# Hybrid encoder trunk: modulation blocks moved from GpSimd to VectorE and TensorE, squares of y kept in pairs, and a mixed block order for the last state-space group

## The chip, the cores and the metric

The kernel runs on one core of a Trainium2 chip. Its time is device time in microseconds (us), the median over runs of the same program. The engines that matter are TensorE (PE, with its weight loads PEld), VectorE (DVE), ScalarE (ACT), GpSimd (POOL), and the queue of SyncE (SP) that issues most transfers. Each engine works through its own instructions in program order, and waits for another engine's results where it needs them.

## The reference, cut to what matters

Two layers over a sequence of 1024 tokens with a width of 1024, in fp32. Layer 0 mixes tokens by dilated window attention with a partial rotary embedding, layer 1 by a bidirectional Mamba-2 state-space mixer of inner width 2048 in eight groups.

```python
cond = silu(c)
for i in range(2):
    mod = cond @ mod_w[i] + mod_b[i]                 # 1024 -> 3072
    shift, scale, gate = split(mod, 3)
    hn = rms_norm(x, norm_w[i]) * (1 + scale) + shift
    if i == 0: y = dilated_attention_mixer(hn, ...)  # (o * silu(z)) @ w_out
    else:      y = bi_ssd_mixer(hn, ...)             # below
    x = x + gate * y
return rms_norm(x, final_norm_w)

# end of bi_ssd_mixer
y = (y_f + y_b + xs * d_skip).reshape(b, s, 2048) * silu(z)
return rms_norm(y, norm_w) @ w_out                   # 2048 -> 1024
```

## The kernel before

Features lie on the 128 partitions and tokens along the free axis, so x is eight tiles (`xt[kt]`) of 128 x 1024. Dense products are made to fp32 accuracy from three matmuls: each operand is split into a high part (a rounded copy, made by ScalarE) and a low part (the difference, made by VectorE), and TensorE sums high x high, high x low, low x high. One such triple (lines 376 to 378 in `mm3`, 1004 to 1006 in `out_items`) covers 128 x 128 weights and 512 tokens. Two triples, for both halves of the tokens, are called a half-step below. The main loop of the kernel is written as lists of such steps, into which the other work is woven.

The start is in `layer0`. The squares of x are made by ScalarE, some are merged by VectorE, and summed over partitions by matmuls with ones, which gives the sum `ss[h]` for each half h of the tokens. From it the inverse root `r[h]` comes as ScalarE's exp(-0.5 ln) and one Newton step on VectorE. The modulation of layer 0 is needed at the same time: shift and scale of feature tile kt are blocks 2kt and 2kt + 1 of 24. A block is a tile of 128 x 1024 (eight 128 x 128 pieces of the modulation weights, `mod_load`). Its product with silu(c), called `cond`, is made before in three stages: all eight pieces are multiplied by their column of `cond` (`mod_acc`; even blocks from 2 on by ScalarE in eight scalings, line 169; blocks 0, 1 and all odd ones by GpSimd in one multiply, line 173), the eight pieces are summed to two (an add of 512 and one of 256 elements, here called a half-sum; on VectorE at line 867 or on GpSimd at line 177), and `mod_fin` sums over the partitions with one-column matmuls (line 197) and forms `modv` and the scale `gs`.

With them `hn_tile` makes the normed tile of a feature tile: x times `gs` times r on VectorE (line 287), the high part with the shift on ScalarE (line 293), the low part on VectorE (line 294). The loop over kt then has eight steps. In each, TensorE makes 18 dense matmuls (three blocks q, k, v of the first head pair, two halves of the tokens, three matmuls each), and the others prepare the tile of the next step, the weights' high and low parts (`w_split`, lines 271 and 272) and modulation blocks of later steps. Loads of modulation blocks stand in the queue of SP two blocks at a time, three pairs ahead of their use.

The tables of the rotary embedding (`rope_tables`) are a long row of small operations of 192 columns. `NT` says how many of them VectorE does at given places of the start. After step 5 of the loop the rest goes to GpSimd.

Layer 1 runs over eight groups. `block_order` sets the order of a group's six projection blocks (x0, x1, B, C and the gates z0, z1); `group_dense` gives a group's projection steps and `ssd_items` those of its scan, a state part (`A1`, `A2`) and then eight chunks (`B0`, `B1`, `M`, `B2`), and `balance` weaves such a list with the projection blocks of the next group, so that each dense half-step stands where the ratio of TensorE's to VectorE's planned time wants it. An item is (length, function, TensorE's us, VectorE's us).

Beside the last group (g = 7) run the first 14 steps of the out-projection (`out1`, `first`) instead of a next group's blocks; such a step has 12 matmuls. Here y is fetched from DRAM tile by tile (`fetch`), and `prep` squares it (ScalarE, or GpSimd for the first three, line 1554), adds the square to a sum on GpSimd (line 1558), and makes the high part (ScalarE, line 1561) and the low part (VectorE, line 1562). The sum of squares over the partitions follows in `sums`. `B2` also ends with gate multiplies on GpSimd (line 1495).

Of the kernel before, what the change touches and what calls it, by code (L numbers as in the profile page):

```python
# [17 lines left out]
P = 128  # L18
# [73 lines left out]
class Trunk:  # L92
# [97 lines left out]
    def mod_fin(self, i, b, *accs):  # L190

        nc = self.nc
        p = self.bank("a2", [P, H2])
        for k, acc in enumerate(accs):
            n = acc.shape[1]
            for c in range(0, n, P):
                nc.tensor.matmul(p[:, k * P:k * P + 1], acc[:, c:c + P], self.ones[:, :1], start=c == 0, stop=c + P == n)
        m = self.modv[i]
        for k in range(len(accs)):
            c = slice(b + k, b + k + 1)  # L200
            nc.vector.tensor_add(m[:, c], p[:, k * P:k * P + 1], self.vec[:, 16 + 24 * i + b + k:17 + 24 * i + b + k])
            if b + k < 16 and (b + k) % 2:
                d = (b + k) // 2
                nc.vector.scalar_tensor_tensor(self.gs[i][:, d:d + 1], m[:, c], 1.0,
                                               self.vec[:, 64 + 8 * i + d:65 + 8 * i + d], op0=OP.add, op1=OP.mult)

# [134 lines left out]
    def block_order(self, g):  # L341

        return (0, 4, 1, 2, 3, 5) if 0 < g < 7 else tuple(range(6))
# [469 lines left out]
    def layer0(self):  # L813
# [33 lines left out]
        self.w_dma(3)  # L847

# [19 lines left out]

        def fin(j):
            self.mod_fin(0, 2 * j, *[mw.pop(2 * j + s)[:, :2 * P] for s in range(2)])  # L870
# [18 lines left out]
        mods(0, nc.gpsimd, 1)  # L889
        mods(1, nc.gpsimd, 1)  # L890
# [24 lines left out]
        fin(0)  # L915
        prep(0)
        self.w_split(1)
        mods(4, nc.scalar)
        mods(5, nc.gpsimd)
        self.finish()  # L920
        self.flush()
        half(2)
        half(4)
        accs = [[self.acc() for _ in range(2)] for _ in range(2)] + [[self.bank("a0", [P, H2], 2) for _ in range(2)]]
        evac = self.evac0 = self.attn_evac(0)
        for kt in range(KT):
            load(kt + 4)
            if 3 < kt + 4 < KT:
                self.w_dma(kt + 4)
            if kt + 3 < KT:  # L930
                mods(2 * kt + 6, nc.scalar)
                mods(2 * kt + 7, nc.gpsimd)
            for m in range(3):
                if m == 0 < kt < KT - 1:
                    fin(kt + 1)
                self.mm3(accs[m], self.whl[kt], slice(m * P, m * P + P), [self.hn[n][kt] for n in range(2)],
                         kt == 0, kt == KT - 1)
                if kt == KT - 1:
# [456 lines left out]
    def ssd_items(self, g):  # L1395
# [119 lines left out]
        if g == 7:  # L1515
            items.append((1500, lambda: None, 0, 0))
# [10 lines left out]
    def out1(self, tail):  # L1527
# [3 lines left out]
        xin, x2, cut, ybuf = {}, {}, {}, {}  # L1531
        ys, st = [{} for _ in range(2)], [{} for _ in range(2)]

        def fetch(r, kt):
            if (r, kt) in cut or (r, kt) in ybuf or kt > 15:
                return
            buf = ybuf[r, kt] = self.big()
            if kt < 14:
                nc.sync.dma_start(buf[:, :H2], self.yd[kt][:, H2 * r:H2 * r + H2])

        def prep(r, kt):
# [67 lines left out]
        def sums(r, a):  # L1609
# [5 lines left out]
            def total():  # L1615
                ys[r]["s"] = self.all_sum(ys[r], 0, H2, self.acc())
# [4 lines left out]
            return [(0.5, out), (1, total), (1, start)]  # L1621

        def first(ps):
            m = tail[0][:]
            for i in range(4):
                m.insert(len(m) - 10 + 2 * i, (1, lambda i=i: prep(0, i)))
            weave(m + [(2600, f) for _, f in ps[0][:14]], tail[1])
            for _, f in ps[1][:2]:
                f()
            for kt in (14, 15):  # L1630
                prep(0, kt)
            for _, f in ps[1][2:4]:
                f()
            self.phase("w3")
# [163 lines left out]
```

## Time and profile before

| | |
|---|---|
| time, median of 3 runs | 1859.21 us (1858.36 to 1860.43) |
| the profiled execution's own time | 1857.47 us |
| its span | 1855.5 us |
| TensorE busy | 1777.3 us (96%) |
| PE weight loads busy | 1453.4 us (78%) |
| VectorE busy | 1420.6 us (77%) |
| ScalarE busy | 956.6 us (52%) |
| GpSimd busy | 328.0 us (18%) |

The busy times are shares of one profiled execution's span. The shares are means over stages of different kinds: a stage in which an engine is nearly always busy can stand beside one in which it waits. So the stages are read one by one, from windows (the busy time of each engine in a stretch) and timelines (an engine's instructions in order; equal ones in a row are joined, and the second number is their time together). Instructions that reach the hardware as several are listed several times: a one-column matmul of the program shows as two. PEclk is the granted clock of TensorE as a share of full speed (2.4 GHz; the lower level is 1.2). "[9.59 <-ACT big L293]" says that the engine was idle for 9.59 us before the instruction, and that the last thing it waited for was ScalarE's write to a tile `big` at line 293.

### The profile page before, as it was taken

To read this page: it belongs to the slowest core of one execution; us is meant where nothing else is said; L and a number is where in the kernel's file an instruction comes from. 1 tells how busy PE (TensorE), PEld (TensorE's weight loads), DVE (VectorE), ACT (ScalarE), POOL (GpSimd) and SP (SyncE) were. 2 spreads that over 40 slices of the span, in tenths; PEclk is the share of its full clock that TensorE was granted. 3 is DMA by queue.
4 is the path that set the end of the run, shared out by engine and by line. 5 is a ranking of instruction groups with operands and counts; after the bars stand their busy time and mean duration, and the time that the engine had idled before them with its cause. 6 is when DMAs were issued, how large, how long until landed. Compare 5 with 4: busy or idle time off the path is not lost.

```text
span 1855.5 us, 28487 instructions
## 1 busy us (share of the span) xinstructions
PE 1777.3 (96%) x10050; PEld 1453.4 (78%) x10050; DVE 1420.6 (77%) x3219; ACT 956.6 (52%) x2095; POOL 328.0 (18%) x493
## 2 busy tenths in 40 slices
PE   5899999999999999999999999999999999798997
PEld 2678788878788888788878788888888878676787
DVE  7966578766755655666687989899898989897975
ACT  5454445544444544544435656565656565565632
POOL 4611112112211221010110101010101010233310
PEclk7899999999999999999999999999999999999998
DMA  6242234322412131173313243433323342344542
GB/s 249 94 122 90 84 103 129 99 84 87 120 47 58 56 80 55 59 229 136 100 41 97 69 118 82 114 89 93 100 83 108 80 111 78 114 133 140 187 160 96
DMA packets 99733, 193.65 MB, mean 104 GB/s; under 512 B 15624, under 2 KB 23048, under 8 KB 99592
## 3 DMA queue, kind: packets, MB, share of 16 engines
q1 hardware_dynamic: 86600, 167.32, 29.7%
q0 software_dynamic: 12288, 23.86, 4.7%
q8 instruction: 79, 1.29, 0.3%
q10 hardware_dynamic: 704, 0.66, 0.1%
q14 instruction: 62, 0.51, 0.1%
HBM read 169.00 MB, written 16.48 MB: 100 GB/s over the span
## 4 chain that ended last, share of the span: by engine, by line
PE 72%; DVE 17%; ACT 4%; issue 3%; DMA 3%; SPq 0%; ACTq 0%; DVEq 0%; POOL 0%
PE acc L376 16%; PE acc L378 15%; PE acc L377 15%; PE a L1487 3%; PE a L1425 2%; DVE wlo L272 2%; PE a L719 2%; PE a L1004 2%; PE a L1005 2%; PE a L1006 2%; DVE big L1336 2%; PE a L704 2%; PE acc L1006 2%; PE acc L1004 2%; PE acc L1005 2%
## 5 line engine op out<-in xcount | busy, mean ns | idle before, releaser
L376 PE MATMUL acc<-big,whi 128*128 128x512 f32 (+1 forms) x1520 | 631.2, 415 | 13.0 <-ACT big L293 12.4
L377 PE MATMUL acc<-big,whi 128*128 128x512 f32 (+1 forms) x1520 | 595.3, 392 | 2.7 <-DVE big L294 2.6
L378 PE MATMUL acc<-big,wlo 128*128 128x512 f32 (+1 forms) x1520 | 595.3, 392 | 0.3 <-DVE wlo L272 0.3
L376 PEld LDWEIGHTS acc<-big,whi 128*128 128x128 f32 x1520 | 288.0, 189 | 78.6 <-issue 15.8
L378 PEld LDWEIGHTS acc<-big,wlo 128*128 128x128 f32 x1520 | 287.5, 189 | 64.3 <-DVE wlo L272 1.2
L377 PEld LDWEIGHTS acc<-big,whi 128*128 128x128 f32 x1520 | 288.7, 190 | 53.0 <-DVE big L294 6.1
L272 DVE TENSOR_TENSOR wlo<-wraw,whi 128x512 fp32r<-128x512 f32 (+1 forms) x297 | 214.1, 726 | 83.1 <-ACT whi L271 80.1
L271 ACT CAST whi<-wraw 128x512 fp32r<-128x512 f32 (+1 forms) x302 | 181.3, 612 | 85.5 <-PE a L1005 27.3
L695 ACT ACTIVATE sm<-sm,nb 128x256 f32<-128x256 f32 (+1 forms) x192 | 89.3, 466 | 194.9 <-DVE nb L693 192.2
L1336 DVE SCALAR_TENSOR_TENSOR big<-acc,cv,big 128x512 f32<-128x512 f32 (+1 forms) x248 | 169.2, 741 | 6.5 <-ACT big L1328 6.5
L1495 POOL TENSOR_TENSOR big<-big,yt 128x128 f32<-128x128 f32 x128 | 65.3, 531 | 586.7 <-DVE yt L1491 586.6
L1457 ACT ACTIVATE E<-E,nacb 128x128 f32<-128x128 f32 x256 | 81.8, 391 | 143.1 <-DVE E L1449 129.4
L706 DVE COPY pt<-a 128x512 f32<-128x512 f32 (+1 forms) x96 | 57.6, 600 | 73.2 <-PE a L704 73.1
L690 DVE CUSTOM_DVE_ANT_0 sm<-a,cst 128x256 f32<-128x256 f32 (+1 forms) x192 | 64.9, 375 | 60.3 <-PE a L685 60.0
L1004 PE MATMUL a<-big,whi 128*128 128x256 f32 (+1 forms) x304 | 99.2, 326 | 0.0
L1006 PE MATMUL a<-big,wlo 128*128 128x256 f32 (+1 forms) x304 | 98.2, 323 | 0.1
L1005 PE MATMUL a<-big,whi 128*128 128x256 f32 (+1 forms) x304 | 97.9, 322 | 0.0
L1005 PE MATMUL acc<-big,whi 128*128 128x512 f32 x224 | 88.9, 397 | 5.9 <-DVE big L1562 3.1
L592 POOL DMA_DIRECT2D rt<-kT x92 | 50.3, 561 | 243.0 <-ACT kT L532 145.8
L1006 PE MATMUL acc<-big,wlo 128*128 128x512 f32 x224 | 89.5, 399 | 3.2 <-DVE wlo L272 2.4
L1004 PE MATMUL acc<-big,whi 128*128 128x512 f32 x224 | 90.5, 404 | 0.0
L1328 ACT ACTIVATE big<-acc,cv 128x512 f32<-128x512 f32 x62 | 44.5, 770 | 86.4 <-PE acc L378 76.0
(254 smaller groups left out, 3181.7 us busy)
## 6 DMA issues: line engine op xcount, KB each, us to landing
wraw<-in_win SPq DMA_DIRECT2D x186, 256.0 KB
acs<-acsd SPq DMA_DIRECT2D x64, 512.0 KB
wraw<-in_wout SPq DMA_DIRECT2D x112, 256.0 KB
big<-in_modw SPq DMA_DIRECT2D x48, 512.0 KB
yd<-big POOLq DMA_DIRECT2D x14, 512.0 KB, 4.4
big<-yd SPq DMA_DIRECT2D x28, 256.0 KB
vT<-mix POOLq DMA_DIRECT2D x20, 256.0 KB, 4.2
big<-in_xT SPq DMA_DIRECT2D x8, 512.0 KB
```

Of the source, the lines that this page charges most:

```text
L271: self.nc.scalar.copy(dst_hi, src)
L272: self.late.append((lambda: self.lo_engine.tensor_sub(dst_lo, src, dst_hi.bitcast(F32)), tile))
L376: mm(o, hi[:, cols], x_[:, t0:t0 + n], start=first, stop=False, **kw)
L377: mm(o, hi[:, cols], x_[:, H2 + t0:H2 + t0 + n], start=False, stop=False, **kw)
L378: mm(o, lo[:, cols], x_[:, t0:t0 + n], start=False, stop=last, **kw)
L695: nc.scalar.activation(sm[:, h, :W], sm[:, h, :W], AF.Exp, bias=nb[:, h:h + 1], scale=0.125, accum_out=stat[:, h, 1, i:i + 1])
L1004: mm(o, hi[:, c], x[:, t:t + n], start=kt == 0 and (n == H2 or m % 2 == 0), stop=False, **kw)
L1005: mm(o, hi[:, c], x[:, H2 + t:H2 + t + n], start=False, stop=False, **kw)
L1006: mm(o, lo[:, c], x[:, t:t + n], start=False, stop=kt == nkt - 1, **kw)
L1336: nc.vector.scalar_tensor_tensor(y[:, lo:hi], a[:, lo + o:hi + o], w[:, cv, k:k + 1], y[:, lo:hi], op0=OP.mult, op1=OP.add)
L1457: nc.scalar.activation(E[:, h], E[:, h], AF.Exp, bias=self.nacb[:, c, 4 * g + h:4 * g + h + 1])
L1495: nc.gpsimd.tensor_mul(z, z, t[:, r])
```

## The change

It has three parts. First, the modulation of layer 0. GpSimd takes no block any more. Block 0 is multiplied and half-summed by VectorE. Blocks 1, 2, 3, 4, 6, 10 and 14 (`pe`) aren't multiplied at all: TensorE multiplies their eight pieces with the eight columns of `cond`, summing over the partitions and the pieces in one go. The other eight (`act`) are scaled by ScalarE and half-summed by VectorE. `mod_fin` gives way to a new `fin`. Two more pairs of blocks are loaded ahead. The order of the start changes too: the first weights' split stands ahead of the norm, and the first half's Newton step and normed tile come before the second half's.

Second, the squares of y for the first half of the tokens. y is fetched in pairs of tiles. ScalarE makes all squares and writes them into pair tiles; GpSimd adds the pair tiles (`add_pair`), three of them inside the list of steps and four behind it; the last sum takes two matmuls. The first four tiles of y are prepared, and the next ones fetched, a few places earlier, and the list is woven by `balance` instead of `weave`. The total is asked for two places later.

Third, the last group's blocks stand in the mixed order of the others, and an empty item of its list gets a planned 2.0 us of VectorE.

```diff
     def block_order(self, g):
 
-        return (0, 4, 1, 2, 3, 5) if 0 < g < 7 else tuple(range(6))
+        return (0, 4, 1, 2, 3, 5) if g else tuple(range(6))
...
+        load(4)
+        load(5)
...
+
         def fin(j):
-            self.mod_fin(0, 2 * j, *[mw.pop(2 * j + s)[:, :2 * P] for s in range(2)])
+
+            p = self.bank("a0", [P, 2, P], 2) if j < 2 else self.bank("a2" if j % 2 else "a3", [P, 2, P])
+            for k in (1, 0):
+                w = mw.pop(2 * j + k)
+                n = KT if 2 * j + k in pe else 2
+                for c in range(n):
+                    x = self.cond[:, c:c + 1] if n == KT else self.ones[:, :1]
+                    nc.tensor.matmul(p[:, k, :1], w[:, c * P:c * P + P], x, start=c == 0, stop=c == n - 1)
+            m = self.modv[0]
+            c = slice(2 * j, 2 * j + 2)
+            nc.vector.tensor_add(m[:, c], p[:, :, 0], self.vec[:, 16 + 2 * j:18 + 2 * j])
+            nc.vector.scalar_tensor_tensor(self.gs[0][:, j:j + 1], m[:, 2 * j + 1:2 * j + 2], 1.0,
+                                           self.vec[:, 64 + j:65 + j], op0=OP.add, op1=OP.mult)
 
         turn(NT[0])
         for kt in range(KT):
...
         for h in range(2):
             merge(6, slice(h * H2, h * H2 + H2))
             total(sq[6], False, True, (h,))
+        mods(0, nc.vector, 1)
+        half(0)
+        self.w_split(0)
+        self.flush()
         r, v = [[self.u(t, [P, H2], F32, n) for _ in range(2)] for t, n in (("pt", 4), ("sm", SM))]
...
-            half(h)
-        self.w_split(0)
-        mods(2, nc.scalar)
-        mods(3, nc.gpsimd)
-        def prep(kt):
+        self.w_split(1)
+
+        def prep(kt, hs=range(2)):
             if kt < KT:
-                for h in range(2):
+                for h in hs:
                     self.hn_tile(0, kt, h * H2, H2, xt[kt][:, h * H2:h * H2 + H2], r[h], self.hn)
 
         for h in range(2):
             nc.vector.scalar_tensor_tensor(u[h], u[h], -0.5, v[h], op0=OP.mult, op1=OP.mult)
             nc.vector.scalar_tensor_tensor(r[h], u[h], 1.5, r[h], op0=OP.add, op1=OP.mult)
-        fin(0)
-        prep(0)
-        self.w_split(1)
-        mods(4, nc.scalar)
-        mods(5, nc.gpsimd)
+            if h == 0:
+                fin(0)
+            prep(0, (h,))
+            self.flush()
...
+        mods(5, nc.scalar)
         self.finish()
         self.flush()
-        half(2)
-        half(4)
+        fin(1)
...
-            load(kt + 4)
+            if kt < 2:
+                load(kt + 6)
...
-                mods(2 * kt + 6, nc.scalar)
-                mods(2 * kt + 7, nc.gpsimd)
...
+            for b in (2 * kt + 4, 2 * kt + 5):
+                if b in act:
+                    half(b)
             prep(kt + 1)
             self.w_split(kt + 2)
+            for b in (2 * kt + 6, 2 * kt + 7):
+                if b in act:
+                    mods(b, nc.scalar)
...
-            items.append((1500, lambda: None, 0, 0))
+            items.append((1500, lambda: None, 0, 2.0))
...
+        def add_pair(k):
+
+            for n in range(2):
+                c = slice(n * H2, n * H2 + H2)
+                nc.gpsimd.tensor_add(pairs[0][:, c], pairs[0][:, c], pairs[k][:, c])
+            pairs[k] = None
...
-            if r == 0 and kt < 3:
-                nc.gpsimd.tensor_mul(sq, y, y)
             else:
-                nc.scalar.activation(sq, y, AF.Square)
-            if kt:
+                sq = buf[:, H2:]
+            nc.scalar.activation(sq, y, AF.Square)
+            if kt and r:
                 nc.gpsimd.tensor_add(ys[r]["sq"][:, :H2], ys[r]["sq"][:, :H2], sq)
...
-            for i in range(4):
-                m.insert(len(m) - 10 + 2 * i, (1, lambda i=i: prep(0, i)))
-            weave(m + [(2600, f) for _, f in ps[0][:14]], tail[1])
+            for at, f, k in ((1, prep, 3), (2, prep, 2), (3, fetch, 4), (4, prep, 1), (6, prep, 0), (8, fetch, 2), (12, fetch, 0)):
+                m.insert(max(len(m) - at, 0), (1, lambda f=f, k=k: f(0, k), 0, 0.7 if f is prep else 0))
+            balance(m + [(2600, f, 2.76, 1.4) for _, f in ps[0][:14]], tail[1])
+            add_pair(4)
+            add_pair(5)
```

How instructions stand on three engines, before and after. VectorE at the start, from the first half-sums to the first normed tile, before (`sm` and `pt` hold the variance and the inverse root, `big_104` and `big_106` are blocks 0 and 1, `kT` is the normed tile):

```order
L867 TENSOR_TENSOR big_104<-big_104 128x512
L867 TENSOR_TENSOR big_104<-big_104 128x256
L900 TENSOR_SCALAR sm_210<-a_14_87 128x512
L867 TENSOR_TENSOR big_106<-big_106 128x512
L867 TENSOR_TENSOR big_106<-big_106 128x256
L913 SCALAR_TENSOR_TENSOR big_211<-big_211,sm_209 128x512
L914 SCALAR_TENSOR_TENSOR pt_207<-big_211,pt_207 128x512
L913 SCALAR_TENSOR_TENSOR big_211<-big_211,sm_210 128x512
L914 SCALAR_TENSOR_TENSOR pt_208<-big_211,pt_208 128x512
L201 TENSOR_TENSOR modv_6_75<-a_50_242,vec_65 128x1 x2
L204 SCALAR_TENSOR_TENSOR gs_8_77<-modv_6_75,vec_65 128x1
L287 SCALAR_TENSOR_TENSOR kT_250<-big_88,gs_8_77,pt_207 128x512
```

And after, the same place:

```order
L173 TENSOR_TENSOR big_104<-big_104,cond_73 128x1024
L852 TENSOR_TENSOR big_104<-big_104 128x512
L852 TENSOR_TENSOR big_104<-big_104 128x256
L255 TENSOR_TENSOR wlo_217<-wraw_108,whi_216 128x384
L903 TENSOR_SCALAR sm_222<-a_13_86 128x512
L903 TENSOR_SCALAR sm_223<-a_14_87 128x512
L914 SCALAR_TENSOR_TENSOR big_224<-big_224,sm_222 128x512
L915 SCALAR_TENSOR_TENSOR pt_220<-big_224,pt_220 128x512
L869 TENSOR_TENSOR modv_6_75<-a_57_240,vec_65 128x2
L870 SCALAR_TENSOR_TENSOR gs_8_77<-modv_6_75,vec_65 128x1
L270 SCALAR_TENSOR_TENSOR kT_253<-big_88,gs_8_77,pt_220 128x512
L255 TENSOR_TENSOR wlo_234<-wraw_114,whi_233 128x384
```

The multiply of block 0 (line 173 in both) is new here, block 1's half-sum is gone, and the first half's Newton step and normed tile stand ahead of the second half's Newton step.

GpSimd at the start, before (`big_104`, `big_106`, `big_112` are blocks 0, 1 and 3):

```order
L173 TENSOR_TENSOR big_104<-big_104,cond_73 128x1024
L173 TENSOR_TENSOR big_106<-big_106,cond_73 128x1024
L173 TENSOR_TENSOR big_112<-big_112,cond_73 128x1024
L177 TENSOR_TENSOR big_112<-big_112 128x512
L177 TENSOR_TENSOR big_112<-big_112 128x256
L173 TENSOR_TENSOR big_118<-big_118,cond_73 128x1024
L177 TENSOR_TENSOR big_118<-big_118 128x512
L177 TENSOR_TENSOR big_118<-big_118 128x256
```

And after, where `vT` and `V` hold the rotary tables:

```order
L464 TENSOR_TENSOR vT_82<-vT_82,vT_83 128x192 x2
L464 TENSOR_TENSOR vT_83<-vT_83 128x192
L471 TENSOR_TENSOR V_84<-V_84,vT_82 128x192 x2
L471 TENSOR_TENSOR V_84<-V_84,vT_83 128x192
L475 TENSOR_SCALAR vT_82<-V_84 128x192
L477 TENSOR_SCALAR vT_83<-vT_82 128x192
L479 TENSOR_SCALAR vT_83<-vT_83 128x192
L481 TENSOR_TENSOR V_84<-vT_82,vT_83 128x192
```

The multiplies are gone, and the rotary tables' second part, which stood behind the last of them, is the first work.

GpSimd in the last group, before, from the first squares (line 1554) and accumulations (line 1558) of y to the first gate multiplies (line 1495):

```order
L1554 TENSOR_TENSOR big_15779<-big_15777 128x512
L1554 TENSOR_TENSOR big_15837<-big_15837 128x512
L1558 TENSOR_TENSOR big_15779<-big_15779,big_15837 128x512
L1554 TENSOR_TENSOR big_15860<-big_15860 128x512
L1558 TENSOR_TENSOR big_15779<-big_15779,big_15860 128x512
L1558 TENSOR_TENSOR big_15779<-big_15779,big_15902 128x512
L1558 TENSOR_TENSOR big_15779<-big_15779,big_15973 128x512
L1558 TENSOR_TENSOR big_15779<-big_15779,big_16022 128x512
L1558 TENSOR_TENSOR big_15779<-big_15779,big_16055 128x512
L1495 TENSOR_TENSOR big_15790<-big_15790,yt_16154 128x128
L1495 TENSOR_TENSOR big_15965<-big_15965,yt_16154 128x128
L1558 TENSOR_TENSOR big_15779<-big_15779,big_16105 128x512
```

And after (line 1556 is now `add_pair`):

```order
L1556 TENSOR_TENSOR big_15878<-big_15878,big_15889 128x512 x2
L1556 TENSOR_TENSOR big_15878<-big_15878,big_15965 128x512 x2
L1495 TENSOR_TENSOR big_15200<-big_15200,yt_16293 128x128
L1495 TENSOR_TENSOR big_15906<-big_15906,yt_16293 128x128
L1556 TENSOR_TENSOR big_15878<-big_15878,big_16061 128x512 x2
L1495 TENSOR_TENSOR big_15200<-big_15200,yt_16363 128x128
L1495 TENSOR_TENSOR big_15906<-big_15906,yt_16363 128x128
L1495 TENSOR_TENSOR big_15200<-big_15200,yt_16430 128x128
L1495 TENSOR_TENSOR big_15906<-big_15906,yt_16430 128x128
L1495 TENSOR_TENSOR big_15200<-big_15200,yt_16494 128x128
```

The squares are gone from GpSimd, and the accumulations are fewer and stand in pairs of instructions.

TensorE at the end of the last group's chunks, before (line 1487 makes the outputs of the last two chunks, from the decayed C tiles `acs`, the states `SS` and the chunk's own part `E`; the `acc` are the out-projection's sums):

```order
L1487 MATMUL a_3041_16598<-acs_16355,SS_15800 64x128 x2
L1487 MATMUL a_3041_16598<-acs_16355,SS_15944 64x128 x2
L1487 MATMUL a_3041_16598<-E_16452,xt_15724 64x128 x2
L1004 MATMUL acc_15969<-big_16475,whi_16480 128x512
L1005 MATMUL acc_15969<-big_16475,whi_16480 128x512
L1006 MATMUL acc_15969<-big_16475,wlo_16481 128x512
L1004 MATMUL acc_15970<-big_16475,whi_16480 128x512
L1005 MATMUL acc_15970<-big_16475,whi_16480 128x512
L1006 MATMUL acc_15970<-big_16475,wlo_16481 128x512
```

And after, the same place (the `a_` sums of line 1004 belong to the next pass of the out-projection):

```order
L1487 MATMUL a_3043_16629<-acs_16460,SS_15876 64x128 x2
L1487 MATMUL a_3043_16629<-acs_16460,SS_16055 64x128 x2
L1487 MATMUL a_3043_16629<-E_16525,xt_15823 64x128 x2
L1487 MATMUL a_3045_16647<-acs_16523,SS_16082 64x128 x2
L1487 MATMUL a_3045_16647<-E_16586,xt_15785 64x128 x2
L1487 MATMUL a_3045_16647<-acs_16523,SS_16082 64x128 x2
L1487 MATMUL a_3045_16647<-E_16586,xt_15785 64x128 x2
L1004 MATMUL a_3047_16666<-big_15880,whi_16446 128x512
L1005 MATMUL a_3047_16666<-big_15880,whi_16446 128x512
L1006 MATMUL a_3047_16666<-big_15880,wlo_16447 128x512
```

The step of the out-projection between the last two chunks has moved ahead: the two stand back to back, and the next pass follows. In the whole program the state part of group 6 has 13 dense half-steps where it had 10, its chunks 35 where they had 31, the state part of group 7 has 14 where it had 13, and the chunks of group 7 have 18 where they had 26.

## Rows read from the trace of the kernel before

**Rows 1.** The page: busy tenths of TensorE in 40 slices.
```profile
PE   5899999999999999999999999999999999798997
```

**Rows 2.** Windows: length, busy PE, PEld, DVE, ACT, POOL (us); PEclk, DMA share, GB/s.
```profile
16.60:30.00 13.40, 5.64 (x17) 3.18 (x15) 11.00 (x11) 6.62 (x16) 12.72 (x7) 0.72 0.80 311
30.00:37.40 7.40, 0.03 (x1) 0.04 (x1) 7.17 (x9) 0.81 (x2) 5.78 (x5) 0.50 0.00 0
43.30:89.00 45.70, 39.70 (x166) 30.68 (x165) 44.30 (x62) 21.59 (x52) 29.84 (x26) 0.86 0.34 121
```

**Rows 3.** Timeline, TensorE: start, us, operation xcount, [idle before <-releaser].
```profile
37.37 0.80 PE L376 MATMUL acc<-big,whi 128*128 128x512 f32 x1 [9.59 <-ACT big L293]
...
39.28 0.79 PE L378 MATMUL acc<-big,wlo 128*128 128x512 f32 x1 [0.34 <-DVE wlo L272]
...
40.73 0.63 PE L378 MATMUL acc<-big,wlo 128*128 128x512 f32 x1
41.16 1.70 PE L197 MATMUL a<-ones,big 128*128 128x1 f32 x8
...
46.99 0.39 PE L378 MATMUL a<-big,wlo 128*128 128x512 f32 x1
47.21 0.95 PE L197 MATMUL a<-ones,big 128*128 128x1 f32 x8
...
93.33 0.39 PE L378 MATMUL a<-big,wlo 128*128 128x512 f32 x1
```

**Rows 4.** Timeline, GpSimd, its first multiplies.
```profile
17.04 6.82 POOL L173 TENSOR_TENSOR big<-big,cond 128x1024 f32<-128x1024 f32 x3 [16.08 <-DMA big<-in_modw]
```

**Rows 5.** Timeline, VectorE, the last merge of squares and the first half-sum.
```profile
16.67 1.28 DVE L859 TENSOR_TENSOR big<-big,big 128x512 f32<-128x512 f32 x2
...
20.85 3.29 DVE L867 TENSOR_TENSOR big<-big 128x512 f32<-128x512 f32 x2
```

**Rows 6.** Timeline, VectorE, a half-sum and a normed tile's products.
```profile
60.83 1.14 DVE L867 TENSOR_TENSOR big<-big 128x512 f32<-128x512 f32 x2
...
62.33 1.41 DVE L287 SCALAR_TENSOR_TENSOR kT<-big,gs,pt 128x512 f32<-128x512 f32 x2
```

**Rows 7.** Timeline, GpSimd, rotary tables, second part: first and last of 17.
```profile
71.28 2.04 POOL L481 TENSOR_TENSOR vT<-vT,vT 128x192 f32<-128x192 f32 x2
...
83.15 0.83 POOL L498 TENSOR_TENSOR V<-vT,vT 128x192 f32<-128x192 f32 x1
```

**Rows 8.** Timeline, VectorE, pairs of 512-wide steps in that time.
```profile
71.80 2.08 DVE L294 SCALAR_TENSOR_TENSOR big<-kT,modv,big 128x512 fp32r<-128x512 f32 x2
...
76.99 1.70 DVE L287 SCALAR_TENSOR_TENSOR kT<-big,gs,pt 128x512 f32<-128x512 f32 x2
```

**Rows 9.** Timeline, VectorE, two low parts of y in the last group.
```profile
1654.12 0.74 DVE L1562 SCALAR_TENSOR_TENSOR big<-big,sv,big 128x512 fp32r<-128x512 f32 x1
...
1661.64 1.76 DVE L1562 SCALAR_TENSOR_TENSOR big<-big,sv,big 128x512 fp32r<-128x512 f32 x1
```

**Rows 10.** Timeline, ScalarE, one step of the start, 63 to 68 us.
```profile
63.11 1.39 ACT L293 ACTIVATE big<-kT,modv 128x512 fp32r<-128x512 f32 x2 [3.69 <-DVE kT L287]
64.40 0.50 ACT L271 CAST whi<-wraw 128x384 fp32r<-128x384 f32 x1
64.81 2.45 ACT L169 ACTIVATE big<-big,cond 128x128 f32<-128x128 f32 x8
```

**Rows 11.** Windows of groups 6 and 7, columns as before.
```profile
1500.00:1600.00 100.00, 94.19 (x587) 75.93 (x584) 92.13 (x201) 59.85 (x139) 11.37 (x25) 0.98 0.31 88
1600.00:1631.50 31.50, 26.67 (x115) 20.78 (x114) 20.77 (x38) 11.82 (x25) 8.52 (x8) 0.95 0.44 126
1631.50:1698.00 66.50, 55.80 (x354) 42.31 (x353) 65.29 (x125) 45.74 (x109) 27.96 (x26) 0.97 0.46 135
```

**Rows 12.** Timeline, GpSimd, an accumulation of squares in the last group.
```profile
1660.90 1.96 POOL L1558 TENSOR_TENSOR big<-big,big 128x512 f32<-128x512 f32 x1 [1.71 <-ACT big L1556]
```

**Rows 13.** Waits, VectorE, 1480 to 1730 us: us in total, times, longest.
```profile
DVE big L1562 <- ACT big L1561: 12.6, 5, 4.2
```

More of the change, by code (lines that the diff above doesn't have):

```diff
@@ L188, in mod_acc @@
             nc.vector.tensor_add(out, acc, odd)
[L190 to L205, printed above, removed]
     def mod_sum(self, i, b, accs):
@@ L888, in layer0 @@
                 turn(NT[1])
-        mods(0, nc.gpsimd, 1)
-        mods(1, nc.gpsimd, 1)
         for h in range(2):
@@ L1530, in out1 @@
         nc, io = self.nc, self.io
-        xin, x2, cut, ybuf = {}, {}, {}, {}
+        xin, x2, cut, ybuf, pairs = {}, {}, {}, {}, []
         ys, st = [{} for _ in range(2)], [{} for _ in range(2)]
@@ L1536, in fetch @@
                 return
-            buf = ybuf[r, kt] = self.big()
-            if kt < 14:
-                nc.sync.dma_start(buf[:, :H2], self.yd[kt][:, H2 * r:H2 * r + H2])
+            if r:
+                buf = self.big()
+                ybuf[r, kt] = buf, buf[:, :H2]
+                if kt < 14:
+                    nc.sync.dma_start(buf[:, :H2], self.yd[kt][:, H2:])
+            elif kt < 14:
+                buf = self.big()
+                for k in range(2):
+                    y = buf[:, H2 * k:H2 * k + H2]
+                    ybuf[r, kt - kt % 2 + k] = buf, y
+                    nc.sync.dma_start(y, self.yd[kt - kt % 2 + k][:, :H2])
+            else:
+                ybuf[r, kt] = None, None
+        def add_pair(k):
[3 more added lines that the diff above has]
+            pairs[k] = None
         def prep(r, kt):
@@ L1545, in prep @@
             fetch(r, kt)
-            buf = ybuf.pop((r, kt))
-            y, sq = buf[:, :H2], buf[:, H2:]
+            buf, y = ybuf.pop((r, kt))
             if kt >= 14:
                 y = self.ylast[kt - 14][:, H2 * r:H2 * r + H2]
-            if kt == 0:
+            if r == 0:
+                if kt % 2 == 0:
+                    pairs.append(self.big())
+                    if kt in (8, 10, 12):
+                        add_pair(kt // 2 - 3)
+                sq = pairs[-1][:, kt % 2 * H2:kt % 2 * H2 + H2]
+            elif kt == 0:
                 ys[r]["sq"] = self.big()
                 sq = ys[r]["sq"][:, :H2]
-            if r == 0 and kt < 3:
-                nc.gpsimd.tensor_mul(sq, y, y)
-            else:
-                nc.scalar.activation(sq, y, AF.Square)
-            if kt:
+            else:
+                sq = buf[:, H2:]
+            nc.scalar.activation(sq, y, AF.Square)
+            if kt and r:
                 nc.gpsimd.tensor_add(ys[r]["sq"][:, :H2], ys[r]["sq"][:, :H2], sq)
@@ L1615, in total @@
             def total():
-                ys[r]["s"] = self.all_sum(ys[r], 0, H2, self.acc())
+                if r:
+                    ys[r]["s"] = self.all_sum(ys[r], 0, H2, self.acc())
+                    return
+                p = ys[r]["s"] = self.acc()
+                for n in range(2):
+                    nc.tensor.matmul(p, self.ones, pairs[0][:, n * H2:n * H2 + H2], start=n == 0, stop=n == 1)
             def start():
                 ys[r]["v"] = self.rstd_start(ys[r]["s"], 2 * D, H2)
-            return [(0.5, out), (1, total), (1, start)]
+            return [(0.5, out)] + [(2, lambda: None)] * (r == 0) + [(1, total), (1, start)]
         def first(ps):
             m = tail[0][:]
-            for i in range(4):
-                m.insert(len(m) - 10 + 2 * i, (1, lambda i=i: prep(0, i)))
-            weave(m + [(2600, f) for _, f in ps[0][:14]], tail[1])
+            for at, f, k in ((1, prep, 3), (2, prep, 2), (3, fetch, 4), (4, prep, 1), (6, prep, 0), (8, fetch, 2), (12, fetch, 0)):
[3 more added lines that the diff above has]
+            add_pair(5)
             for _, f in ps[1][:2]:
@@ L1631, in first @@
                 prep(0, kt)
+            add_pair(6)
             for _, f in ps[1][2:4]:
                 f()
+            add_pair(7)
             self.phase("w3")
```

6 lines of the change are left out of this document (1 added, 5 removed).

## The prediction

> **What bounds the kernel now.** I read the page's slices first, for where TensorE falls short. Its digits are nines except in slices 1, 2, 35, 37 and 40 [rows 1]. So there are two places: the start, before the first layer's dense matmuls run freely, and the last group of the second layer with the out-projection woven in. Between them lies a TensorE-bound body that shifts as a whole when the start gets shorter.
>
> The windows show the start as VectorE's [rows 2]: from 16.6 to 37.4 us TensorE works 5.7 us of 20.8 and VectorE 18.2; from 43.3 to 89 us VectorE is busy 44.3 of 45.7 us, and TensorE's granted clock is 0.86 of 2.4 GHz. The first dense matmul starts at 37.37 us after 9.59 us of idling, and the wait for the low weights ends at 39.28 [rows 3]. VectorE is slow because GpSimd works beside it: GpSimd multiplies three modulation blocks from 17.04 to 23.86 us [rows 4]; beside that a half-sum (an add of 512, one of 256) takes 3.29 us [rows 5]. Later the same half-sum takes 1.14 us and two 512-wide steps 1.41 [rows 6].
>
> **The start, step by step.** All modulation multiplies leave GpSimd: nine large ones and their 14 adds. Block 0 goes to VectorE, seven blocks to TensorE as matmuls against the silu vector, eight to ScalarE. But GpSimd doesn't fall silent. The second part of the rotary tables stood behind the multiplies and is now its first work; it can begin when VectorE's last table step is done, before VectorE's merges, so at about 16.7 us. Before, it ran from 71.28 to 83.98 us, 12.7 us [rows 7], so it covers the new start until about 29. Beside it two 512-wide steps on VectorE took 2.08 us in its first part (factor 1.5 against 1.41) and 1.70 in the rest (1.2) [rows 8]. I use these factors.
>
> VectorE's merges end at 17.95 us (16.67 + 1.28 [rows 5]). From there: 0.6 for the merges' stretching. The multiply of block 0 (1024 wide) isn't in the trace on VectorE; the nearest rows bound it by 1.41 (two 512-wide steps alone) and 2.3 (6.82 / 3, GpSimd's own); I take 1.9, 1.41 with factor 1.35. Half-sum 1.14 x 1.4 = 1.6. Low part of the first weight, 384 wide, three quarters of the 0.74 of a 512-wide low part [rows 9], x 1.5 = 0.8. Two variance and two Newton steps 4 x 0.7 x 1.2 = 3.4. Modulation add and scale, tiny ones: 0.4, an estimate at half a step. Normed tile 0.85. That is 9.5 us, so 27.5; ScalarE's high part adds 0.7 (1.39 for two [rows 10]): first dense matmul near 28.2. The second half's Newton, normed tile and high part come after it, 1.7 + 0.85 + 0.7: free running from 31.4 us. TensorE's one-column matmuls fit before: the trace shows eight for a pair of blocks summed to two columns each, in 1.70 us at half clock and 0.95 at full [rows 3]; a block with eight columns takes 16, so blocks 0 to 3 are 4 + 3 x 16 = 52, 11 us at half clock, from about 20 us on. Against 39.3 before, the start has gained 8 us.
>
> Then come eight steps of 18 dense matmuls. Their spacing is 0.43 us at half clock (40.73 to 41.16) and 0.22 at full (46.99 to 47.21) [rows 3]: 7.7 or 4.0 us. The first runs at half clock and ends near 39.1. TensorE alone would end the other seven at 39.1 + 7 x 4.0 + 4 x 2.4 + 2 x 0.95 = 78.6 us (four pairs with 20 one-column matmuls, two with 8). ScalarE and VectorE hold them longer: from one step's high parts to the next lie weight cast 0.5, eight scalings 2.45, half-sum 1.14, normed tile 0.75, high parts 1.39 [rows 6, 10], 6.3 us; 8.7 where ScalarE scales two blocks; about 4 where none. From high parts at 33 us three loops of the first kind, two of the second and two of the last end at 77.3, and the last step 4 us later: 81.4. Before, the last matmul of the eighth step ended at 93.7 [rows 3]. That is 12 us; I take 10, since short waits in each step may cost clock. Bounds: 4 (half of the early start kept, each step half a microsecond above its old mean, (93.7 - 39.3) / 8 = 6.8) and 16 (TensorE's 78.6, and no harm from the rotary work).
>
> Four block loads are issued earlier, behind everything that is needed early. I give them nothing: the transfer engines moved nothing from 30 to 37.4 us (DMA share 0.00 [rows 2]).
>
> **The last group, step by step.** In the stretch of its eight chunks, 1631.5 to 1698 us, VectorE is busy 65.29 of 66.5 us: it is the bound, and TensorE idles 10.7 [rows 11]. VectorE loses work there in two ways. By the new order eight low parts of 0.74 us (three of y, five of weights) go ahead of the stretch: 5.9 us. And ten accumulations on GpSimd become six, since squares stay in pairs and the other adds come after the stretch; beside such an add of 1.96 us [rows 12] a low part took 1.76 instead of 0.74 [rows 9], 1.0 each: 4 us. So -9.9.
>
> What went ahead costs elsewhere. Eight dense half-steps left the stretch, six matmuls or 1.3 us each. Seven land between 1500 and 1600 us, 9.2 us of TensorE's time, where it idles 5.8 and VectorE 7.9 of 100 [rows 11]: little is hidden, I charge +7. One lands in the state part of group 7 (1600 to 1631.5), where TensorE idles 4.8 and VectorE 10.7 us, mostly behind high parts whose y was fetched late: 12.6 us in all [rows 13]. The fetches now stand six to eight steps ahead, and three squares leave GpSimd: -3.5. Sum -6.4, taken as -6. Bounds: -15 (the stretch's 9.9 and half of the 12.6, with the moved matmuls hidden) and +5 (the chunks stay as long, and half or more of the 9.2 is paid). The normalizing sum with two matmuls for one and the wait item ahead of it lie beside dozens of dense half-steps: nothing, and 1.3 us if TensorE stands still for one.
>
> **The sum.** The profiled execution took 1857.5 us, 1.7 below the median of the runs. 1857.5 - 10 - 6 = 1841.5; from the median it is 1843. I predict 1842 us.
>
> **A rule weighed.** Rows 6 and 8 show a pair of two-input steps on VectorE stretched from 1.41 to 2.08 us beside the rotary work. The Trainium skill, page "SBUF — State Buffer", section "SBUF: two separate sides", says that VectorE with two SBUF inputs and GpSimd share one port pair under an exclusive lock that holds for a whole instruction. By it each two-input step could wait for a whole GpSimd instruction, while in my sum it loses a fifth to a half of its own length; that is the second rival, and the trace so far leans to the smaller loss.
>
> **The rivals.** First: the last group gives nothing. For it: the moved matmuls land where both engines are 92 to 94% busy. Against: the bound stretch really loses VectorE work. 1859.2 - 10 = 1849 us.
>
> Second: the rotary work eats the start. Nine VectorE instructions, each behind a GpSimd one of 1.0 us (2.04 / 2 [rows 7]), lose 9 us instead of the 3 that I count, and with three more for clock lost in the wait the start gives 1 us: 1859.2 - 1 - 6 = 1852.
>
> Third, on the other side: TensorE's clock stays at half (1.2 GHz) in the start's steps, where one-column matmuls and waits of 1 to 3 us alternate. A step is then 7.7 + 20 x 0.2125 = 11.9 us, 5.5 above the 6.4 at full clock. It decides from four steps on: 22 us undo both gains and 3.7 more. With all eight, +44: 1886 us. For it: the clock was 0.72 from 16.6 to 30, 0.50 from 30 to 37.4, and 0.86 in the steps. Against: in those steps VectorE, not TensorE, was full, and the clock still came up.
>
> Fourth: the waits shift and nothing gets shorter, the loop of ScalarE and VectorE being as long as the old step: 1859 us.
>
> **How the numbers follow.** Both parts pay: 62%, 1829 to 1851. First rival 14%, second 10%, third 7%, fourth 7%. A measurement of this kernel tells 0.2%, 3.7 us, from no change. Faster: 62 + 14 + 10 = 86%; within: 7%; slower: 7%. The range 1829 to 1855 holds the first three but for a few per cent at each end.
>
> **What would show it.** Right: the first dense matmul near 28 us and free running from 31; no multiply on GpSimd at the start but the rotary work at 17 to 29 us; the eighth step ending near 82; the last group's chunk stretch near 57 us, with fewer low parts of 1.7 us, and group 6 some 7 us longer. Wrong: steps of 11 to 12 us with the clock at 0.5 after 45 us, TensorE waiting for half-sums ahead of its one-column matmuls, VectorE steps of 2 us and more before 29 us, or a chunk stretch of 66 us again.

## The result, and the profile after

| | before | after |
|---|---|---|
| median of 4 runs | 1859.82 us | 1834.93 us (1831.87 to 1836.34) |
| ratio, 95% interval | | 0.9862 (0.9844 to 0.988) |
| span of the profiled execution | 1855.5 us | 1830.0 us |

24.9 us faster in the medians, 25.5 in the spans of the two profiled executions. The forecast was 1842 us, 17 below before; the time lies inside its range, below its point. TensorE's slices, as in [rows 1], dip only at the very start and in two late slices:

```profile
PE   8999999999999999999999999999999999997997
```

The start after, TensorE's timeline (answers to [rows 3]):

```profile
20.43 1.84 PE L866 MATMUL a<-cond,big 128*128 128x1 f32 x16
22.14 0.58 PE L866 MATMUL a<-ones,big 128*128 128x1 f32 x4
22.58 6.54 PE L866 MATMUL a<-cond,big 128*128 128x1 f32 x32
28.99 0.77 PE L359 MATMUL acc<-big,whi 128*128 128x512 f32 x1
...
79.85 0.39 PE L361 MATMUL a<-big,wlo 128*128 128x512 f32 x1
```

The 52 one-column matmuls run without a gap into the first dense one. The eighth step ends at 80.2 us, before at 93.7. For the end of the program both spans are cut at the same instructions: the last outputs of group 5's chunks, then the end of each state part and of each chunk stretch. Windows before (columns as in [rows 2]), then after:

```profile
1509.21:1532.49 23.28, 22.51 (x107) 17.97 (x108) 17.10 (x35) 11.21 (x27) 1.94 (x4) 1.00 0.52 147
1532.49:1595.52 63.03, 58.29 (x380) 47.51 (x378) 62.14 (x140) 38.78 (x90) 6.35 (x14) 0.97 0.25 72
1595.52:1626.18 30.66, 25.53 (x113) 19.75 (x114) 21.90 (x39) 11.92 (x30) 9.78 (x10) 0.94 0.48 137
1626.18:1696.83 70.65, 59.95 (x374) 45.69 (x372) 66.76 (x129) 48.69 (x111) 26.85 (x24) 0.98 0.44 131
```

```profile
1492.50:1515.74 23.24, 22.94 (x114) 19.13 (x114) 17.06 (x35) 11.51 (x27) 1.93 (x4) 1.00 0.43 125
1515.74:1581.80 66.06, 66.06 (x422) 54.12 (x421) 63.49 (x141) 40.78 (x94) 6.81 (x14) 1.00 0.33 92
1581.80:1613.38 31.58, 27.12 (x113) 21.07 (x114) 24.39 (x42) 20.23 (x43) 7.58 (x8) 0.89 0.50 158
1613.38:1670.58 57.20, 45.46 (x326) 37.51 (x324) 55.26 (x125) 41.10 (x99) 9.43 (x16) 0.97 0.48 134
```

The account, in us of span: to the end of the eighth step -13.5; from there to the end of group 5 -3.2 (1415.5 to 1412.3); group 6's state part 0, its chunks +3.0; group 7's state part +0.9, its chunks -13.4; the rest +0.7. Sum -25.5. In the last stretch GpSimd falls from 26.85 to 9.43 us and VectorE from 66.76 to 55.26, and VectorE is still the fullest engine.

The 3.2 us in the body have one place in these two profiles. Timeline and windows of TensorE in the first attention unit before, then after:

```profile
124.51 0.38 PE L684 MATMUL a<-K,Q 128*128 128x256 f32 x1 [2.43 <-DVE stat L690]
...
124.50:128.00 3.50, 3.49 (x11) 2.81 (x12) 2.68 (x11) 2.60 (x9) 0.00 (x0) 0.54 0.60 220
```

```profile
109.34 0.39 PE L667 MATMUL a<-K,Q 128*128 128x256 f32 x1 [0.96 <-DVE stat L673]
```

TensorE idled 2.43 us there and ran 3.5 us at 0.54 behind it; after, it idles 0.96 and the clock stays at 1.00. That this is the change's is not shown. With the old start and the new last group (below) TensorE idles 2.34 us and the clock holds; with the new start and the old last group it idles 2.35 us, and the body lasts 1415.2 us, 0.3 less than before.

### The profile page after: what moved, and what is told of

It is laid out like the page before. It is cut to its first block, busy times and chain, and to the rows that moved or that the text cites. A ratio compares the mean times of both kernels' runs of the same rounds, so it can differ in the third digit from the quotient of the medians.

```text
span 1830.0 us, 28629 instructions
## 1 busy us (share of the span) xinstructions
PE 1778.0 (97%) x10136; PEld 1463.5 (80%) x10136; DVE 1395.2 (76%) x3212; ACT 961.9 (53%) x2107; POOL 283.2 (15%) x466
## 4 chain that ended last, share of the span: by engine, by line
PE 83%; DVE 10%; ACT 4%; issue 2%; DMA 1%; SPq 0%; ACTq 0%; DVEq 0%; POOL 0%
PE acc L359 17%; PE acc L361 16%; PE acc L360 16%; PE a L1487 4%; PE a L1425 3%; PE a L1004 3%; PE a L1005 3%; PE a L1006 3%; PE acc L1006 2%; PE a L702 2%; PE acc L1004 2%; PE acc L1005 2%; PE a L687 2%; DVE big L1336 1%; DVE wlo L255 1%
## 5 line engine op out<-in xcount | busy, mean ns | idle before, releaser
L1495 POOL TENSOR_TENSOR big<-big,yt 128x128 f32<-128x128 f32 x128 | 61.6, 502 | 633.7 <-DVE yt L1491 633.7
L1471 DVE SCALAR_TENSOR_TENSOR W<-cb,dt,W 128x128 f32<-128x128 f32 x256 | 85.1, 388 | 8.1 <-ACT W L1459 6.1
```

The source lines that it names most:

```text
L1471: nc.vector.scalar_tensor_tensor(W[:, h], cb[:, 1], self.dt[:, c, hh:hh + 1], W[:, h], op0=OP.mult, op1=OP.add)
```

## The experiments

Times are medians of four executions; beside them the kernel before was timed again (medians of 1858.6 to 1859.0).

**The start alone, the last group alone.** The diff split in two: `layer0` with its helpers, against `block_order`, the planned item and `out1`. For the start alone, shortened (`out1` also has its old text):

```diff
-        return (0, 4, 1, 2, 3, 5) if g else tuple(range(6))
+        return (0, 4, 1, 2, 3, 5) if 0 < g < 7 else tuple(range(6))
...
-            items.append((1500, lambda: None, 0, 2.0))
+            items.append((1500, lambda: None, 0, 0))
```

> The changed start with the last group and the out-projection as before. Theory (the two parts add up): the start gives 13.5 us by the end of the eighth step and 3.1 more at 121 to 130 us, where TensorE's idle time of 2.43 us and the half clock after it go, so about 16.6 us below the kernel before, 1843 us, and the last group lasts as before (the chunk stretch 70.6 us from the end of its last state matmuls to its last outputs). Rival (the gain of the last group is the start's, handed down through transfers or a better phase): 1835 us, all of it.

> The start as before, with the changed last group and out-projection. Theory: about 9 us below the kernel before, 1850 us; the eighth step ends at 93.7 us, and TensorE still idles 2.4 us near 124 us. Rival as for the start alone: no change, 1859 us.

Measured: 1843.6 and 1849.3, that is -15.3 and -9.6; together -24.9. The parts add up, and both rivals fall. One step of the start's theory fails in its trace: the eighth step ends at 79.2 us, and the 3.1 us at the first attention unit don't come (2.35 us of idling, as said above).

**Plain order.**

```diff
-        return (0, 4, 1, 2, 3, 5) if g else tuple(range(6))
+        return (0, 4, 1, 2, 3, 5) if 0 < g < 7 else tuple(range(6))
```

> The changed kernel with the last group's blocks in plain order again (pairs, early fetches and the planned 2.0 us kept). Theory A (the mixed order moves VectorE's work and eight dense half-steps out of the chunk stretch): most of the 9.5 us goes, the chunk stretch is 66 to 70 us, and the time is 1841 to 1844 us. Theory B (the pairs and the fetches carry the gain, by GpSimd's shorter work): the chunk stretch stays under 60 us and the time within 2 us of 1835.

Measured: 1834.3, so theory A falls by its time, and theory B by its stretch. Windows of this kernel at the same cuts:

```profile
1494.56:1517.81 23.25, 22.48 (x107) 17.96 (x108) 17.09 (x35) 11.20 (x27) 1.94 (x4) 1.00 0.59 148
1517.81:1580.54 62.73, 58.05 (x380) 47.48 (x379) 61.85 (x140) 38.52 (x90) 6.38 (x14) 0.97 0.26 72
1580.54:1603.26 22.72, 22.01 (x107) 18.00 (x108) 17.75 (x35) 13.33 (x33) 3.06 (x5) 1.00 0.71 197
1603.26:1671.91 68.65, 59.76 (x380) 48.11 (x378) 63.22 (x133) 49.08 (x112) 15.47 (x20) 0.95 0.49 135
```

The mixed order takes 11.4 us out of the last stretch (68.65 to 57.20) and puts 3.3 into group 6's chunks and 8.9 into group 7's state part. It moves the work and wins nothing: +0.7 us by these windows, and the same by the medians.

**The pairs alone** of the last group's edits, with the changed start.

```diff
-            balance(m + [(2600, f, 2.76, 1.4) for _, f in ps[0][:14]], tail[1])
+            for i in range(4):
+                m.insert(len(m) - 10 + 2 * i, (1, lambda i=i: prep(0, i)))
+            weave(m + [(2600, f) for _, f in ps[0][:14]], tail[1])
```

> The changed start; of the last group's edits the pairs alone (plain order, the four tiles of y prepared where they were, the list woven by the old rule, no planned 2.0 us). Theory (pairs and early placing carry about half of the last group's gain each): 1839 us, between the start alone (1843.6) and the plain order with both (1834.3); the state part of group 7 stays at 30 to 32 us, the chunk stretch falls by 4 to 6 us from 70.6. Rival 1 (pairs carry all): 1834 us. Rival 2 (placing carries all): 1843 us.

Measured: 1839.0, as the theory has it: 4.6 from the pairs (against 1843.6), 4.7 from early placing, `balance` and the planned 2.0 us together (1834.3). The stretches lie a little off: state part 28.5 us, chunk stretch 67.0, 3.6 less.

**Single adds.** Every square is added by itself as it comes, in place of `add_pair`, which is not called (shortened).

```diff
...
+            elif kt:
+                nc.gpsimd.tensor_add(pairs[0][:, :H2], pairs[0][:, :H2], sq)
```

> The changed kernel with every square added by itself on GpSimd as it comes (14 more adds of 512 in all, none behind the list), all squares still on ScalarE and the order mixed. Theory B: each add inside the stretch stretches a VectorE step by 1.0 us, 5 to 6 of them come back, 1839 to 1841 us. Theory A: VectorE has slack between its waits and the time stays within 1.5 us of 1835.

Measured: 1839.0, +4.1. Its last stretch (window), two of its seven stretched VectorE steps and GpSimd's adds beside them (timelines):

```profile
1614.55:1677.50 62.95, 48.52 (x326) 39.15 (x324) 60.68 (x125) 41.66 (x100) 20.60 (x22) 0.91 0.47 125
...
1642.79 1.76 DVE L1584 SCALAR_TENSOR_TENSOR big<-big,sv,big 128x512 fp32r<-128x512 f32 x1
1650.25 1.76 DVE L1584 SCALAR_TENSOR_TENSOR big<-big,sv,big 128x512 fp32r<-128x512 f32 x1
...
1642.04 1.96 POOL L1580 TENSOR_TENSOR big<-big,big 128x512 f32<-128x512 f32 x1 [1.70 <-ACT big L1576]
1649.57 1.90 POOL L1580 TENSOR_TENSOR big<-big,big 128x512 f32<-128x512 f32 x1 [1.77 <-ACT big L1576]
```

Seven VectorE steps of 1.75 to 1.79 us stand there, where 0.68 to 0.75 is their length alone. The changed kernel has none, only one group of four small steps that takes 3.47 us beside a pair add where 1.36 is usual:

```profile
1633.17 3.47 DVE L1471 SCALAR_TENSOR_TENSOR W<-cb,dt,W 128x128 f32<-128x128 f32 x4
...
1633.88 2.63 POOL L1556 TENSOR_TENSOR big<-big,big 128x512 f32<-128x512 f32 x2
```

Seven times 1.05 less 2.1 is 5.3 us; VectorE's busy time is 5.4 us longer, the stretch 5.7. So the adds that came out of the stretch are the pairs' gain.

**Six blocks back on GpSimd** at the start (shortened; the line for block 5 changes alike).

```diff
-                    mods(b, nc.scalar)
+                    mods(b, nc.gpsimd if b % 2 else nc.scalar, 1)
```

> The changed kernel with the six odd ScalarE blocks (5, 7, 9, 11, 13, 15) multiplied by GpSimd as before, the half-sums still on VectorE. Theory (GpSimd's multiplies stretch VectorE's steps beside them by a half and more, and that was the old start's length): VectorE's pairs of normed-tile steps take 2 to 3 us again in place of 1.41 in the stretch that GpSimd works in, the eighth step ends 4 to 10 us later than 80.2, and the time is 1838 to 1845 us. Rival (the gain is ScalarE's and TensorE's shorter chain, GpSimd's multiplies are hidden): within 1.5 us of 1835, or below, since ScalarE loses six blocks of 2.45 us.

Measured: 1838.1, +3.1, at the theory's lower edge. Its times (1835.9 to 1839.8) touch those of the changed kernel (1831.9 to 1836.3), so the trace has to tell: the eighth step ends at 84.2 us, against 78.5 to 81.0 in the six profiles that have the changed start as it is. GpSimd, then VectorE in its timeline:

```profile
27.74 1.90 POOL L173 TENSOR_TENSOR big<-big,cond 128x1024 f32<-128x1024 f32 x1 [1.82 <-DMA big<-in_modw]
...
36.57 1.95 POOL L173 TENSOR_TENSOR big<-big,cond 128x1024 f32<-128x1024 f32 x1 [0.88 <-DMA big<-in_modw]
...
27.83 2.35 DVE L915 SCALAR_TENSOR_TENSOR pt<-big,pt 128x512 f32<-128x512 f32 x1
...
36.68 3.05 DVE L270 SCALAR_TENSOR_TENSOR kT<-big,gs,pt 128x512 f32<-128x512 f32 x2
```

A step of 0.69 us took 2.35, a pair of 1.41 took 3.05: the GpSimd multiply of 1.9 us costs the VectorE step that begins beside it 1.65. Each of the six multiplies lengthens one VectorE step so, by 1.5 to 1.7 us. The price in time is net of the six blocks that ScalarE loses, and 4.0 us at the eighth step is less than a third of the start's 13.5. What block 0 on VectorE, the seven blocks on TensorE and the earlier loads carry of the rest was not taken apart.

**The rotary work held back.**

```diff
+                hold = self.u("hold", [P, 1])
+                nc.gpsimd.tensor_copy(hold, self.modv[0][:, 6:7])
                 self.rope_engine = nc.gpsimd
```

> The changed kernel with the rotary tables' second part on GpSimd held back by a tiny copy that waits for the modulation of the fourth feature tile (near 44 us). Theory (at the first dense matmul TensorE's own 52 one-column matmuls end last, VectorE's loss beside GpSimd is covered): the first dense matmul stays at 28.5 to 29 us, VectorE's second normed tile is ready 1.5 to 2.5 us sooner, and the time is 1834 to 1838 us, since the rotary work now stretches VectorE's steps near 44 to 58 us, which are on the path. Rival (each two-input step of VectorE waits for whole GpSimd instructions there): the first dense matmul moves to 25 to 26 us and the time to 1829 to 1831 us.

Measured: 1835.0, no change. VectorE in the start of the changed kernel, then here:

```profile
18.59 1.70 DVE L852 TENSOR_TENSOR big<-big 128x512 f32<-128x512 f32 x2
...
28.20 1.62 DVE L277 SCALAR_TENSOR_TENSOR big<-kT,modv,big 128x512 fp32r<-128x512 f32 x2
```

```profile
18.70 1.15 DVE L852 TENSOR_TENSOR big<-big 128x512 f32<-128x512 f32 x2
...
26.39 1.62 DVE L277 SCALAR_TENSOR_TENSOR big<-kT,modv,big 128x512 fp32r<-128x512 f32 x2
```

All of the rotary work cost VectorE 1.8 us up to the second half's normed tile (28.20 to 26.39). The first dense matmul did move, to 25.9, against the theory; but so it did, to 26.1, in the profile of the spread tiles below, whose start is the changed kernel's own. There the clock fell later (0.88 from 23 to 26 us, against 0.51), and the second dense matmul waited for VectorE's low part instead:

```profile
26.11 0.80 PE L359 MATMUL acc<-big,whi 128*128 128x512 f32 x1
29.10 0.80 PE L360 MATMUL acc<-big,whi 128*128 128x512 f32 x1 [2.19 <-DVE big L277]
```

So the changed start has two ends close together, TensorE's one-column matmuls and VectorE's low parts, and TensorE runs free from 29 us by either. With the rotary work held back the eighth step ends at 78.3 us, which one execution of the changed start reaches as well (78.5); no gain shows in the time.

**Both halves' Newton steps first**, as before.

```diff
-            if h == 0:
-                fin(0)
-            prep(0, (h,))
-            self.flush()
+        fin(0)
+        prep(0)
+        self.flush()
```

> The changed kernel with the Newton steps of both halves ahead of both normed tiles, as before. Theory (the first dense matmul waits for TensorE's one-column matmuls at half clock until 29 us, and the second half's high part was ready at 29.0 as well): first dense matmul within 1 us of 29, time within 1 us of 1835. Rival (the order of the halves carries part of the start's gain): 1837 us or more.

Measured: 1835.0, first dense matmul at 28.95. The order of the halves is worth nothing here.

**One ScalarE block a step.**

```diff
-        pe, act = (1, 2, 3, 4, 6, 10, 14), (5, 7, 8, 9, 11, 12, 13, 15)
+        pe, act = (1, 2, 3, 4, 6, 8, 10, 12, 14), (5, 7, 9, 11, 13, 15)
```

> The changed kernel with blocks 8 and 12 on TensorE too, so that ScalarE scales one block in every step of the start. Theory (the loop of ScalarE and VectorE holds the steps in which ScalarE scales two blocks: high parts at 39.7, 48.1, 54.2, 62.5, 68.6 us, 8.4 us with two and 6.1 with one): the eighth step ends near 76.5 us, not 80.2, and the time is 1831 us. Rival (TensorE is the bound by then, 16 more one-column matmuls in two steps cost 3 us): 1835 us or more.

Measured: 1835.0, the rival. Windows of the changed kernel, then of this one:

```profile
45.00:60.00 15.00, 14.71 (x72) 12.04 (x71) 10.56 (x21) 11.15 (x34) 0.00 (x0) 0.91 0.11 36
60.00:75.00 15.00, 14.29 (x67) 11.60 (x66) 11.75 (x22) 8.41 (x20) 0.00 (x0) 0.87 0.12 35
```

```profile
45.00:60.00 15.00, 15.00 (x81) 12.97 (x80) 9.83 (x20) 8.25 (x22) 0.00 (x0) 0.89 0.12 37
60.00:75.00 15.00, 15.00 (x87) 13.07 (x87) 11.27 (x21) 8.69 (x18) 0.00 (x0) 1.00 0.13 35
```

TensorE had 1 us of idle time left to give, in 30; the eighth step ends at 79.3, not 76.5, and inside the 78.5 to 81.0 of the changed start.

**The first tiles of y spread out.**

```diff
-            for at, f, k in ((1, prep, 3), (2, prep, 2), (3, fetch, 4), (4, prep, 1), (6, prep, 0), (8, fetch, 2), (12, fetch, 0)):
+            for at, f, k in ((1, prep, 3), (4, prep, 2), (6, fetch, 4), (8, prep, 1), (11, prep, 0), (15, fetch, 2), (18, fetch, 0)):
```

> The changed kernel with the first four tiles of y prepared two dense half-steps apart, and fetched four to six earlier, in place of all four ahead of the last half-step. Theory (in the state part of group 7 TensorE waits 2.6 us for ScalarE's copy of the last gate, which stands behind four tiles' squares and high parts, and runs at half clock after it): the state part of group 7 falls from 31.6 to 27 us or less and the time to 1830 to 1832 us. Rival (the transfers of y or the buffers hold the tiles, or the part is bound by TensorE's state matmuls and VectorE): 1834 to 1836 us.

Measured: 1835.5. My theory falls: the state part lasts 32.1 us. ScalarE was free in time, but TensorE's state matmuls now waited for VectorE; the tiles had only changed places with other work:

```profile
1592.25 2.08 PE L1425 MATMUL a<-xd,bt 128*128 128x256 f32 x4 [2.95 <-DVE xd L1424]
```

**Three edits together** (plain order, one ScalarE block, rotary work held).

> The changed kernel with three of the single edits together: plain order of the last group (alone 1834.3), one ScalarE block a step (alone 1835.0) and the rotary work held back (alone 1835.0, first dense matmul 25.9 us). Theory (the start is now bound by TensorE, and what is won there waits for the rotary transfers and VectorE near 86 to 109 us, so single gains don't show): the eighth step ends 2 to 4 us sooner than 80.2, and the time is 1832 to 1835 us, no clear gain over the changed kernel. Rival (the single gains were each blocked by the other, together they count): 1829 us or less.

Measured: 1831.0 (1830.4 to 1831.6), ratio to before 0.985 (0.9835 to 0.9864): a little below my theory and short of the rival. The eighth step ends at 78.95 us, 1.3 sooner and not 2 to 4. Its runs lie under those of the changed kernel, but the two intervals overlap; whether the 3.9 us are more than noise, and which edit carries them, is open. It has the lowest median here.

## Why the prediction was right, point by point

**The start: right, undersized, one count lucky.** Forecast: first dense matmul at 28.2, TensorE free from 31.4, 8 us sooner than 39.3. Measured: first dense matmul at 29.0 and free from there, -10.3. VectorE's chain was shorter than my sum: merges not stretched (done at 17.42), the multiply of block 0 in 1.21 us, under my lower bound of 1.41, and the first normed tile at 25.3, not 27.5. There it was GpSimd that gave way, in its timeline, against the 2.04 of [rows 7]:

```profile
15.96 4.04 POOL L464 TENSOR_TENSOR vT<-vT,vT 128x192 f32<-128x192 f32 x2 [14.99 <-DVE vT L461]
```

TensorE's one-column matmuls ended last in this profile, 8.6 us for 52 where I had 11. I had called them covered, though my own numbers (11 us from about 20) end at 31, behind the 28.2.

The loop of ScalarE and VectorE was spaced as worked out. Its high parts in ScalarE's timeline

```profile
33.26 1.39 ACT L276 ACTIVATE big<-kT,modv 128x512 fp32r<-128x512 f32 x2 [1.88 <-DVE kT L270]
...
39.71 1.39 ACT L276 ACTIVATE big<-kT,modv 128x512 fp32r<-128x512 f32 x2 [2.31 <-issue]
...
48.07 1.39 ACT L276 ACTIVATE big<-kT,modv 128x512 fp32r<-128x512 f32 x2 [1.88 <-DVE kT L270]
...
54.17 1.35 ACT L276 ACTIVATE big<-kT,modv 128x512 fp32r<-128x512 f32 x2 [1.96 <-DVE kT L270]
...
73.19 1.34 ACT L276 ACTIVATE big<-kT,modv 128x512 fp32r<-128x512 f32 x2 [2.80 <-DVE kT L270]
```

stand 6.45, 8.36 and 6.1 us apart (forecast 6.3 and 8.7). But from 33 us on there are six such loops, not the seven that I added: the last high parts stand at 73.2, not 77.3. And the loop hardly held TensorE, against what I had written: from 29.0 to 80.2 us TensorE was busy 50.2 of 51.2. It took 4 us more than the 47.2 that I gave its own work (78.6 less 31.4): 1.0 us of idling, and some 3 us beside which the clock was low (0.53 from 57 to 60 us, 0.67 from 63 to 66). So the eighth step's end at 80.2, near my 81.4, is partly luck: a loop too many stood in for what TensorE lost with the clock. The 3.2 us of the first attention unit I had not seen, and they are not shown to be the change's: the idle time there varies between executions of one start (0.4 to 2.35 us in these profiles).

**The last group: right in direction, undersized, and its net partly luck.** -6 forecast, -9.6 measured. Pairs: -4 forecast, 4.6 and 4.1 measured. Placing: -3.5 forecast, 4.7 measured, and in the place that I had named: in plain order it brings the state part of group 7 from 28.5 to 22.7 us. Mixed order: -5.9 and +7 forecast, a net of +1.1; measured +0.7 by the medians. There both halves were far too small, 11.4 us out and 12.2 in, and their errors cancelled. Nor did I put the cost where it fell: group 6's chunks pay 3.3 of it, and the state part of group 7 pays 8.9, which hides the placing's gain. What holds TensorE there is a wait for ScalarE's copy of the last gate, which the mixed order puts behind four tiles of y; in plain order that wait is absent (TensorE's timeline after):

```profile
1597.37 0.79 PE L1004 MATMUL acc<-big,whi 128*128 128x512 f32 x1 [2.58 <-ACT big L1348]
```

**A rule weighed.** Beside GpSimd's multiplies a VectorE step lost 1.65 of 1.9 us, as the Trainium skill ("SBUF — State Buffer", "SBUF: two separate sides") has it: the loser waits for a whole instruction. My factors of 1.2 and 1.5 were wrong in kind for such multiplies, and so was the reading that the trace leaned to the smaller loss. The second rival, built on the rule, still failed by its count: nine such waits didn't come, the rotary work cost VectorE 1.8 us in all. Most of its instructions take 0.6 to 1.1 us, and a pair of them waited itself (4.04 us above); that this is the reason is argued, not tested.

**The other rivals.** The first fell by the last group alone (-9.6). The third: the clock was 0.51 from 23 to 26 us and 0.65 from 29 to 35.2, but 0.92 over the seven steps behind. The fourth fell with the result.

## What to carry to other kernels

What GpSimd's elementwise work costs is read from the VectorE steps that begin beside it, by count: here one multiply of 1.9 us cost one step up to 1.7 us, one add cost one step 1.05 us, and a row of instructions of mostly 0.6 to 1.1 us cost 1.8 us in all. A sum that lands near the measured end can still have the wrong engine in it: count what the trace shows waiting. An order that moves work out of a full stretch is judged over all stretches that receive it; here it moved 11 us and won none. When a stage has two bounds close together, easing one of them shows nothing.

## What the runs showed of the hardware

TensorE's clock fell amid one-column matmuls that followed each other without a gap: 16 of them took 1.84 us, 4 took 0.58, the next 32 took 6.54. The windows of the changed kernel count the engine as busy throughout, while the granted clock goes from 1.00 to 0.51:

```profile
20.00:23.00 3.00, 3.00 (x26) 2.75 (x24) 2.81 (x5) 2.86 (x5) 2.78 (x5) 1.00 1.04 406
23.00:26.00 3.00, 3.00 (x16) 3.00 (x16) 2.90 (x7) 1.74 (x4) 2.73 (x4) 0.51 1.03 404
```

The moment of the fall is not fixed by the program: with the same start, the profile of the spread tiles has 0.88 from 23 to 26 us, and there the 32 take 4.04 us.
